# A decoder layer on one core: the pool mixer's map as a plain float32 product, and the kernel's plan with other factors by stage

## The chip, the cores and the metric

The kernel runs on one core of a Trainium2 chip, in one launch. The metric is the device time of an execution in microseconds. Three runs of the kernel before gave 1251.17, 1251.86 and 1253.36 us; their median is 1251.86. One more execution was profiled: its time is 1254.77 us, and its span, from the first to the last recorded instruction, 1252.9 us. All readings of the profile are from that one.

The engines are named PE (matrix products; PEld its weight loads), DVE (vector), ACT (scalar functions), POOL (a second vector engine, which also issues the accumulating transfers) and SP (issues the other transfers). Each has its own queue of instructions and runs it in order.

## The reference

One layer of a hybrid decoder for a prompt of 1024 tokens and 8 single tokens of other sequences (1032 columns in all), everything in float32, D = 1024:

```python
h = rmsnorm(x, g_mix)
u = h @ w_in                                    # a (512), val (512), gate (512)
ya = pool_mixer(a_ext, ...)                     # see below
yb = conv_mixer(val * sigmoid(gate), ...)       # depthwise width 31, LayerNorm, silu
x = x + concat([ya, yb]) @ w_out
x = x + cross_attn(rmsnorm(x, g_attn), mk, mv)  # 4 heads, 256 memory tokens; mk, mv = rmsnorm(mem) @ w_k, w_v
x = x + (silu(h @ w_gate) * (h @ w_up)) @ w_down   # h = rmsnorm(x, g_ffn)
```

The pool mixer, which the change touches, has four groups of 128 channels with trailing windows of 2, 4, 8 and 16 tokens:

```python
for g, w in enumerate((2, 4, 8, 16)):
    outs.append(win_sum[g] / minimum(w, pos + 1) - a[g])
y = einsum('blgc,gcd->blgd', d, w_map)          # a 128 x 128 map for each group
y = (y + b_map) * scale
```

The outputs are the final normalised states, the new pooling and convolution states, and the memory keys and values. The 8 single tokens attend to caches of their own, `cache_k` and `cache_v`.

## The kernel before

**Precision.** The kernel gives PE operands of the type float32r. To hold float32 accuracy it splits nearly every operand into a high and a low part, and every product is three products: high by high, high by low, low by high (`PASSES`, and `step3`, L449, with its matmuls at L457). Columns go in three pieces of 344, so one 128-channel block times one 128-row weight block is 9 matmuls of 344 columns. `split` (L338) makes the high part on ACT or POOL (L346 and L348) and the low part, operand minus high part, on DVE or POOL (L357). For weights there is another way, `split_by_dma` (L364): ACT makes the high part and its negated copy (L368; POOL can, L370), and then a transfer that POOL issues (L375) adds the weight from memory to the copy. POOL issues this transfer only when it reaches it in its queue.

**Weights.** They come as numbered blocks, `raw0`, `raw1`, ..., each loaded by SP into one of three buffers (tag "raw") and split into `w0`, `w1`, .... A raw buffer is free again once all parts of the split that read it are done, and only then can the block three further on be loaded. `NOT_BY_DMA` lists the blocks that are split by the engines, `LEAD` says how many blocks ahead the load and the split of a kind of weight are.

**Stages around the change.** The text `ORDER` names the pieces of the first half in the order in which their tasks are made. After the input projection PE runs the memory keys (`keys`, letters K) and values (`values`, V): K0 and K1 give `kT0`, V1 and V0 give `vv1` and `vv0`, K2 and K3 give `kT1`. Each takes two or four weight blocks: w12 to w15 for K0 and K1, w16 to w19 for V1, w20 to w23 for V0, w24 and w25 for K2. This text calls K2 the third key group. The pool mixer (`windows`, W, L777, and `mixer_out`, M, L841) is laid among them: the window sums `win` in doubling steps on DVE or POOL, the mean on DVE (L802 to L804), the split of the result `dop` (L807, L808), on PE the product `pmap` with the map, which is weight block 26 of the ring above, on ACT the evacuation `yf` (L848) with bias and scale, and its split `opa`. Then `oa` multiplies `opa` by the first rows of w_out, and `ob` the convolution's results `opb` by the others.

Later come the queries, and the attention: scores `sc`, softmax `probs`, their transposes `pt` and `pT`, the product with the values `pv`, whose results are evacuated as `oo` (high part on ACT, L1062, low part on DVE, L1063, in two pieces of 512 columns). Between them DVE does the attention of the 8 single tokens, as dot products with the cache (L1097), named `spcache_k3_0_4` and so on for keys or values, head, half and first token, with the broadcast query or probability row `sbcache`, and a small softmax (`sst`, `prow`). `po` (w_o times `oo`) follows, then the feed-forward in gated stages, its down projections, and the last stage.

**What sets the order.** No order of instructions is written out. Every piece of work is a task, `add(engines, emit, r, w)`: the engines that may do it, each with a cost in microseconds, and what it reads and writes. `Program.order()` then plays the tasks through: again and again it takes the engine that can start earliest, and on it the ready task of the highest priority (the one made first, by and large), and notes when the task ends, by its cost. Buffers are part of it: 2 PSUM buffers for the large products (tag "mm"), 3 raw, 2 w, 3 scratch, 19 operands. A group that needs a buffer gets the one that comes free first. So the costs decide which engine does a task and in which place of its queue it stands; on the chip the queues then run in the order that came out, whatever the real times are.

The costs of the kernel before are formulas in columns (`act`, `dve`, `pool_tt`, `pool_ts`) and single numbers for PE; from the down projections on, DVE's base is raised:

```python
fixed["DVE"] = 0.148
```

## Time and profile before

| what | us |
|---|---|
| median of three runs | 1251.86 |
| profiled execution | 1254.77 |
| its span | 1252.9 |
| PE busy | 1215.9 (97%) |
| DVE busy | 926.7 (74%) |
| ACT busy | 529.7 (42%) |
| POOL busy | 458.8 (37%) |

A row of a timeline gives the start in us from the span's start, the duration, the engine, the line, the operation, and what it writes and reads, with buffer numbers left out; "x9" means nine instructions in a row. A bracket tells how long the engine had been idle before, and which instruction or transfer ended that. In the rows of stretches stand the stretch, PE's busy time with its count, the granted TensorE clock (1.00 is full), the share of the transfer engines, and GB/s. "DMA to landing" is the time from a transfer's issue to its last byte.

### The profile page before, as it was taken

Reading aid. Unit: us, or ns where it says so; the run is one execution under the profiler, and the core shown is the slowest. Engines: PE = TensorE matmul, PEld = TensorE weight load, DVE = VectorE, ACT = ScalarE, POOL = GpSimd, SP = SyncE. Lnnn points to the kernel's source line nnn. Section 1 sums busy time; section 2 is a strip of 40 time slices with the busy share of each in tenths; the row PEclk is TensorE's granted clock in tenths of the full one; section 3 lists DMA queues with packets and bytes.
Section 4 is the critical chain, followed back from the end, with each engine's and each line's share of the span. In section 5 each row is a group of like instructions: output and inputs, shape, how many; then the busy total and the mean of one; then the engine's idle time right before and its main releaser. Section 6 shows DMA issues by size and latency. Waiting matters only on the chain.

```text
span 1252.9 us, 22090 instructions
## 1 busy us (share of the span) xinstructions
PE 1215.9 (97%) x8958; PEld 1194.3 (95%) x8958; DVE 926.7 (74%) x1564; ACT 529.7 (42%) x731; POOL 458.8 (37%) x407
## 2 busy tenths in 40 slices
PE   8999996999999999999999999999999999999996
PEld 8999976999999879999999999999999999999996
DVE  7899988657367777679778677866867887778644
ACT  7766648454223453344322222222222364433644
POOL 3577841021101002113422233133324477778401
PEclk9999997999999999999999999999999999999998
DMA  7447686734255664231331332223322597778703
GB/s 281 104 84 169 142 241 177 213 88 163 104 194 207 238 225 169 102 132 38 112 126 60 111 110 102 104 67 111 106 85 89 205 312 198 206 181 206 175 26 111
DMA packets 59157, 183.86 MB, mean 147 GB/s; under 512 B 7920, under 2 KB 11696, under 8 KB 57776
## 3 DMA queue, kind: packets, MB, share of 16 engines
q1 hardware_dynamic: 52288, 157.74, 36.4%
q0 software_dynamic: 6768, 24.72, 11.2%
q8 instruction: 70, 1.15, 0.4%
q14 instruction: 31, 0.25, 0.1%
HBM read 148.80 MB, written 33.64 MB: 146 GB/s over the span
## 4 chain that ended last, share of the span: by engine, by line
PE 73%; DVE 10%; issue 7%; DMA 5%; ACT 2%; POOL 2%; SPq 0%; DVEq 0%; POOLq 0%; ACTq 0%
PE pr L1290 45%; PE ps L457 11%; PE fd L1587 6%; PE oa L457 4%; PE ob L457 4%; DVE cacc L663 2%; DMA raw<-in_w_v 2%; PE sc L1000 1%; DVE spcache_v L1097 1%; DMA spcache_k<-in_cache_k 1%; POOL w L357 1%; PE pv L1058 1%; DVE spcache_k L1097 1%; DMA w<-in_w_in 1%; DVE xss L384 1%
## 5 line engine op out<-in xcount | busy, mean ns | idle before, releaser
L1305 DVE TENSOR_TENSOR su<-pr,su 128x258 f32<-128x258 f32 (+1 forms) x204 | 109.3, 558 | 71.0 <-PE pr L1290 69.9
L1290 PE MATMUL pr<-ab,wTa 128*128 128x258 f32 x1056 | 134.2, 283 | 0.8 <-DVE su L1305 0.8
L1290 PE MATMUL pr<-ab,wG 128*128 128x258 f32 x1056 | 133.9, 283 | 0.8 <-ACT wU L346 0.8
L1290 PEld LDWEIGHTS pr<-ab,wTa 128*128 128x128 f32 x1056 | 130.1, 189 | 1.0 <-issue 1.0
L1290 PEld LDWEIGHTS pr<-ab,wG 128*128 128x128 f32 x1056 | 129.8, 189 | 1.2 <-ACT wU L346 1.1
L1290 PE MATMUL pr<-ab,wTb 128*128 128x258 f32 x1056 | 130.6, 283 | 0.0
L1290 PEld LDWEIGHTS pr<-ab,wTb 128*128 128x128 f32 x1056 | 128.6, 190 | 0.0
L457 PE MATMUL ps<-xop,w 128*128 128x344 f32 x720 | 114.1, 320 | 0.3 <-DMA w<-in_w_in 0.3
L457 PEld LDWEIGHTS ps<-xop,w 128*128 128x128 f32 x720 | 113.3, 188 | 0.6 <-DMA w<-in_w_in 0.6
L1290 PE MATMUL pr<-hb,dV 128*128 128x258 f32 x768 | 98.5, 284 | 1.1 <-ACT pp L1309 0.7
L1290 PEld LDWEIGHTS pr<-hb,dV 128*128 128x128 f32 x768 | 95.0, 189 | 1.8 <-ACT pp L1309 0.9
L457 PE MATMUL ps<-xq,w 128*128 128x344 f32 x576 | 94.8, 321 | 0.0
L457 PE MATMUL po<-oo,w 128*128 128x344 f32 x576 | 91.0, 320 | 0.4 <-DVE oo L1063 0.4
L457 PEld LDWEIGHTS po<-oo,w 128*128 128x128 f32 x576 | 90.7, 188 | 0.7 <-DVE oo L1063 0.7
L457 PEld LDWEIGHTS ps<-xq,w 128*128 128x128 f32 x576 | 90.6, 188 | 0.1
L1305 DVE TENSOR_TENSOR x<-pr,x 128x516 f32<-128x516 f32 (+1 forms) x122 | 63.3, 556 | 23.2 <-PE pr L1290 22.0
L663 DVE SCALAR_TENSOR_TENSOR cacc<-glu,vec,cacc 128x511 f32<-128x511 f32 (+14 forms) x116 | 77.0, 742 | 0.0
L1290 PE MATMUL pr<-hb,dW 128*128 128x258 f32 x576 | 75.0, 283 | 0.2 <-DVE x L1305 0.2
L1290 PEld LDWEIGHTS pr<-hb,dW 128*128 128x128 f32 x576 | 71.7, 189 | 0.4 <-DVE x L1305 0.4
L1587 PE MATMUL fd<-ho,w 128*128 128x258 f32 x576 | 70.0, 283 | 0.0
L346 ACT ACTIVATE w<-raw 128x1024 fp32r<-128x1024 f32 (+2 forms) x34 | 31.6, 932 | 90.2 <-issue 38.2
L1587 PEld LDWEIGHTS fd<-ho,w 128*128 128x128 f32 x576 | 69.5, 189 | 0.1
(323 smaller groups left out, 2338.5 us busy)
## 6 DMA issues: line engine op xcount, KB each, us to landing
gr<-in_w_gu SPq DMA_DIRECT2D x44, 512.0 KB, 3.4
hs<-hb SPq DMA_DIRECT2D x28, 516.0 KB, 4.2
hb<-su SPq DMA_DIRECT2D x8, 1032.0 KB, 4.9
dr<-in_w_dn SPq DMA_DIRECT2D x16, 512.0 KB, 6.2
hb<-hb POOLq DMA_DIRECT2D x12, 516.0 KB, 7.8
spcache_k<-in_cache_k SPq DMA_DIRECT2D x12, 512.0 KB, 5.0
raw<-in_w_in SPq DMA_DIRECT2D x10, 512.0 KB, 5.3
w<-in_w_in POOLq DMA_DIRECT2D x9, 512.0 KB, 6.6
```

What stands on the lines that cost most here:

```text
L346: e.activation(dst(0), src(), AF.Copy, scale=1.0 if gain is None else gain)
L357: e.tensor_tensor(dst(1), src(), f32(dst(0)), ALU.subtract)
L384: add({"Pool": pool_tt(n), "DVE": dve(n)}, lambda e: e.tensor_tensor(total(), total(), sq[:, i, :n], ALU.add), [(sq, i), tkey], [tkey], lo ...
L457: e.matmul(ps[:, c, :CW], w[:, wi, cols], x[:, xi, c * CW : (c + 1) * CW], start=first and p == 0, stop=last and p == 2)
L663: e.scalar_tensor_tensor(acc[h][:, n:], src[:, : HALF - n], w, acc[h][:, n:], ALU.mult, ALU.add)
L1000: e.matmul(bank()[:, i * NMEM : (i + 1) * NMEM], qop[2 * h + dt][:, qi, tt * P : (tt + 1) * P], kk[:, ki, 2 * (h % 2) + dt], start=(dt == ...
L1058: e.matmul(ps[:, c], v[:, vi, m, col : col + P], pT[h][m][:, pi, sl], start=(m == 0 and p == 0), stop=(m == 1 and p == 2))
L1097: e.scalar_tensor_tensor(piece[:, b], piece[:, b], 1.0, bc[:, b], ALU.mult, ALU.mult, accum_out=out(m)[:, first + b : first + b + 1])
L1290: e.matmul(bank(c), w[:, wi, cols(j)], xs[0](j, xi)[:, c * TQ : (c + 1) * TQ], start=j == 0 and p == 0, stop=j == nj - 1 and p == 2)
L1305: from_sums(sums, "DVE", dve, lambda e, src, sl: e.tensor_tensor(as_banks(o(sl), src), src, as_banks(a(sl), src), ALU.add), [akey], [okey])
L1587: e.matmul(view(i), w[:, wi, col : col + P], hops[k][:, xi, lo + i * width // count : lo + (i + 1) * width // count], start=(k == 0 and p ...
```

## The change

The pool map is loaded once, by SP, into a buffer `wmap` of its own, and not split; it is no longer a block of the weights' ring, so every later block's number is one lower. The window results are not split either: `mixer_out` multiplies `win` by `wmap` as float32, with 3 matmuls of 344 columns for a group where it had 9. The evacuation `yf` and its split `opa` stay.

The plan's costs are written in another way: `pe` and `pe32` give PE's costs by columns, `MARGINS` scales or raises costs by the stage in which a task is made (early, gated, down, last), and POOL's base for two-operand work is 0.14 in place of 0.09. `ORDER` holds the same letters, in other lines. `BY_DMA` names, for each kind of weight, the blocks that are split with a transfer; apart from the map they are the ones that the old list left.

```diff
-NOT_BY_DMA = (0, 1, 2, 16, 18, 19, 22, 23, 26, 27, 35, 36, 53, 54)
-BY_DMA = ("w_in", "w_k", "w_v", "pool_map", "w_out_a", "w_out_b", "w_dn", "w_dn2")
+BY_DMA = {"w_in": (2, 3, 4, 5, 6, 7, 9, 10, 11), "w_k": (0, 1, 2, 3, 4, 5, 7), "w_v": (0, 1, 5), "w_out_a": (0, 1, 2, 3), "w_out_b": (0, 1), "w_dn": (17, 18, 19), "w_dn2": (1,)}
-LEAD = {"w_k": 4, "w_v": 3, "pool_map": 1, "w_out_a": 3, "w_q": 5, "w_in": 2, "w_out_b": 5, "w_o": 5}
+LEAD = {"w_k": 4, "w_v": 3, "w_out_a": 3, "w_q": 5, "w_in": 2, "w_out_b": 5, "w_o": 5}
...
+MARGINS = {
+    "early": {"PE": (0.93, 0.0)},
+    "gated": {},
+    "down": {"DVE": (1.0, 0.083)},
+    "last": {"PE": (0.93, 0.0), "DVE": (1.0, 0.083)},
+}
...
-        t.engines = engines
+        t.engines = {}
+        for e, cost in engines.items():
+            factor, more = self.margin.get(e, (1, 0)) if not nbytes else (1, 0)
+            t.engines[e] = cost * factor + more
...
+    def pe(n, count=1):
+        return (0.006 + 0.00044 * n) * count
+
+    def pe32(n):
+        return 0.01 + 0.0017 * n
...
     def pool_tt(n):
-        return 0.09 + 0.00216 * n
+        return 0.14 + 0.00216 * n
...
+    wmap = op_buf("wmap", (P, 512))
...
+        if not dops:
+            dma(lambda: wmap[:], lambda: io["pool_map"][0], 512 * 512, w=[(wmap,)])
...
-        dops[g] = op_r(f"dop{g}")
-        split(lambda p: dops[g][:, p], lambda p: (dops[g], p), cur, T, [ck])
+        dops[g] = cur, ck
...
-        if not opa:
-            state["wm"] = w_take("pool_map")
-        wmap, wmk = state["wm"]
         ps = mm_buf(f"pmap{g}")
-        step3(ps, wmap, wmk, block_cols(g), dops[g], 0, True, True)
+        cur, ck = dops[g]
+
+        def emit(e):
+            for c in range(NCH):
+                e.matmul(ps[:, c, :CW], wmap[:, block_cols(g)], cur()[:, c * CW : (c + 1) * CW], start=True, stop=True)
+
+        add({"PE": NCH * pe32(CW)}, emit, [(wmap,), ck], all3(ps))
...
-            fixed["DVE"] = 0.148
+            pg.margin = MARGINS["down"]
```

Other costs mean another order on every engine. PE's list is nearly the same (one map product stands one group later, a few small swaps); POOL's, ACT's and DVE's are changed in many places. Three of them follow.

**POOL, where the weights of K1, V1 and V0 are made ready.** A row is a line of the code, an operation, what it writes and what it reads; "DMA w17<-in_w_v" is the accumulating transfer of block 17, L357 (now L371) a low part. Before:

```order
L375 DMA w17_1544<-in_w_v 128x1024
L357 TENSOR_TENSOR w18_1565<-raw18_1486,w18_1565 128x1024
L357 TENSOR_TENSOR kT0_1640<-kf0_1628,kT0_1640 128x512
L357 TENSOR_TENSOR w19_1598<-raw19_1547,w19_1598 128x1024
L375 DMA w20_1622<-in_w_v 128x1024
L375 DMA w21_1699<-in_w_v 128x1024
L375 DMA w24_1760<-in_w_k 128x1024
```
Now:

```order
L371 TENSOR_TENSOR kT0_1651<-kf0_1627,kT0_1651 128x512
L389 DMA w17_1538<-in_w_v 128x1024
L371 TENSOR_TENSOR w18_1555<-raw18_1470,w18_1555 128x1024
L371 TENSOR_TENSOR w19_1596<-raw19_1542,w19_1596 128x1024
L389 DMA w20_1620<-in_w_v 128x1024
L371 TENSOR_TENSOR kT0_1651<-kf1_1697,kT0_1651 128x512
L389 DMA w21_1695<-in_w_v 128x1024
L371 TENSOR_TENSOR w22_1735<-raw22_1699,w22_1735 128x1024
L371 TENSOR_TENSOR w23_1746<-raw23_1712,w23_1746 128x1024
L371 TENSOR_TENSOR vv1_1802<-vf1_1787,vv1_1802 128x1024
L389 DMA w24_1764<-in_w_k 128x1024
```
The low part of `kT0` from `kf0` now stands ahead of block 17's transfer, where it stood behind it; that from `kf1` has come to POOL, ahead of block 21's; and the low parts of blocks 22 and 23 (DVE's before) are on POOL, and with `vv1`'s they stand ahead of block 24's transfer, which stood right behind block 21's.

**DVE, the mixer's last results, on the way to the first `oa`.** `win2` are the window sums of a group and then, by L804 (now L818), its mean; `opa` are the low parts of the mixer's results, `y2` and `ysum` the convolution's. Before, from the mean of `win2`:

```order
L804 SCALAR_TENSOR_TENSOR win2_1943<-win2_1943,a1_523 128x1032
L357 TENSOR_TENSOR w27_1947<-raw27_1774,w27_1947 128x1024
L357 TENSOR_TENSOR dop2_2018<-win2_1943,dop2_2018 128x1032
L357 TENSOR_TENSOR opa3_1995<-yf3_1976,opa3_1995 128x1032
L646 TENSOR_TENSOR y2_1082<-y2_1082,cp_593 128x507
L357 TENSOR_TENSOR opa1_2013<-yf1_2007,opa1_2013 128x1032
L646 TENSOR_TENSOR y2_1082<-y2_1082,cp_593 128x506
L682 TENSOR_TENSOR ysum_1203<-ysum_1203,y2_1082 128x1032
L646 TENSOR_TENSOR y2_1082<-y2_1082,cp_593 128x505
L357 TENSOR_TENSOR opa0_2030<-yf0_2015,opa0_2030 128x1032
L831 TENSOR_TENSOR kf3_2106<-kps3_2023,side_206 128x512
```
Now, from the low part of `opa3`:

```order
L371 TENSOR_TENSOR opa3_1975<-yf3_1969,opa3_1975 128x1032
L816 TENSOR_TENSOR win2_1971<-win2_1971,cnt_74 128x2x8
L817 TENSOR_REDUCE win2_1971<-side_206 128x8
L818 SCALAR_TENSOR_TENSOR win2_1971<-win2_1971,a1_523 128x1032
L657 TENSOR_TENSOR y2_1026<-y2_1026,cp_593 128x506
L371 TENSOR_TENSOR opa1_1983<-yf1_1980,opa1_1983 128x1032
L657 TENSOR_TENSOR y2_1026<-y2_1026,cp_593 128x505
L693 TENSOR_TENSOR ysum_1482<-ysum_1482,y2_1026 128x1032
L657 TENSOR_TENSOR y2_1026<-y2_1026,cp_593 128x504
L371 TENSOR_TENSOR opa0_2018<-yf0_2004,opa0_2018 128x1032
```
The low part of `dop2` is gone from between the mean and the results, as those of the three other groups are from further up, and `opa3` is ahead of the mean. Further up, the new list has from the third key group's end `kf2`, the sums of `win0`, the first of `win2`, the mean of `win0`, two more sums of `win2` (the second one was POOL's) around the low part of `kT1`, and then the rows above; in the old list the sums and the mean of `win0` came before `kf2`.

**DVE, the end of the attention.** `oo7` and `oo6` are the low parts of the last two products `pv`, the long names dot products with the cache. Before:

```order
L1097 SCALAR_TENSOR_TENSOR spcache_k3_0_4_4358,ssc_81<-spcache_k3_0_4_4358,sbcache_k3_4_4344 128x256 x4
L1097 SCALAR_TENSOR_TENSOR spcache_k3_1_4_4369,ssc_81<-spcache_k3_1_4_4369,sbcache_k3_4_4344 128x256 x4
L1063 TENSOR_TENSOR oo7_4403<-pv7_4385,oo7_4403 128x512 x2
L1118 TENSOR_REDUCE sst3_4443<-ss3_4431 8x1
L1119 SCALAR_TENSOR_TENSOR sst3_4443<-sst3_4443,r16_78 8x1
L1063 TENSOR_TENSOR oo6_4415<-pv6_4396,oo6_4415 128x512 x2
L1126 RECIPROCAL sst3_4443<-sst3_4443 8x1
L1127 TENSOR_SCALAR prow3_4447<-prow3_4447,sst3_4443 8x256
L1097 SCALAR_TENSOR_TENSOR spcache_v2_0_0_4252,os_80<-spcache_v2_0_0_4252,sbcache_v2_0_4417 128x256 x8
```
Now:

```order
L1079 TENSOR_TENSOR oo7_4359<-pv7_4349,oo7_4359 128x512
L1113 SCALAR_TENSOR_TENSOR spcache_v2_0_0_4208,os_80<-spcache_v2_0_0_4208,sbcache_v2_0_4329 128x256 x8
L1113 SCALAR_TENSOR_TENSOR spcache_k3_0_4_4333,ssc_81<-spcache_k3_0_4_4333,sbcache_k3_4_4320 128x256 x4
L1113 SCALAR_TENSOR_TENSOR spcache_k3_1_4_4336,ssc_81<-spcache_k3_1_4_4336,sbcache_k3_4_4320 128x256 x4
L1113 SCALAR_TENSOR_TENSOR spcache_v2_1_0_4211,os_80<-spcache_v2_1_0_4211,sbcache_v2_0_4329 128x256 x4
L1134 TENSOR_REDUCE sst3_4408<-ss3_4405 8x1
L1135 SCALAR_TENSOR_TENSOR sst3_4408<-sst3_4408,r16_78 8x1
L1113 SCALAR_TENSOR_TENSOR spcache_v2_1_0_4211,os_80<-spcache_v2_1_0_4211,sbcache_v2_0_4329 128x256 x4
L1142 RECIPROCAL sst3_4408<-sst3_4408 8x1
L1143 TENSOR_SCALAR prow3_4417<-prow3_4417,sst3_4408 8x256
L1079 TENSOR_TENSOR oo7_4359<-pv7_4349,oo7_4359 128x512
L1079 TENSOR_TENSOR oo6_4386<-pv6_4368,oo6_4386 128x512 x2
```
The second low part of `oo7` stood behind the dots of `k3`; it now stands behind those and the sixteen dots of `v2`, and the small softmax of head 3.

38 lines of the change are left out of this document (18 added, 20 removed), and 8 rows, old and new, of the table ORDER.

## The prediction

> **What bounds the kernel now.** I read the page first, then TensorE's own line of work, then what the engines that feed it did in its gaps.
>
> ```profile
> PE 1215.9 (97%) x8958; PEld 1194.3 (95%) x8958; DVE 926.7 (74%) x1564; ACT 529.7 (42%) x731; POOL 458.8 (37%) x407
> ```
>
> PE is busy for 97% of 1252.9 us, so 37 us at most can be won by filling its gaps, and everything else must come from less PE work. The question is only where PE stands still, and where it will stand still under the other order. The timeline of PE (start, duration, group, and in brackets the idle time ahead of it with what ended it) shows the gaps that the edit can reach:
>
> ```profile
> 115.83 33.31 PE L457 MATMUL ps<-xop,w 128*128 128x344 f32 x210 [0.30 <-DMA w<-in_w_in]
> 160.44 22.27 PE L901 MATMUL vps<-w,memg 128*128 128x512 f32 x96
> 187.98 2.86 PE L827 MATMUL kps<-memg,w 128*128 128x256 f32 x22 [1.86 <-DMA w<-in_w_k]
> 193.22 1.83 PE L457 MATMUL pmap<-dop,w 128*128 128x344 f32 x9 [2.37 <-ACT vf L906]
> 199.95 5.31 PE L457 MATMUL pmap<-dop,w 128*128 128x344 f32 x18 [4.91 <-ACT yf L848]
> 205.10 2.99 PE L827 MATMUL kps<-memg,w 128*128 128x256 f32 x24
> 215.84 15.80 PE L457 MATMUL oa<-opa,w 128*128 128x344 f32 x81 [3.02 <-ACT yf L848]
> 231.48 1.88 PE L868 MATMUL mean_ps<-ysum,ones_c 128*128 128x512 f32 x4
> 268.22 45.36 PE L457 MATMUL ob<-opb,w 128*128 128x344 f32 x288
> ...
> 430.76 3.03 PE L1058 MATMUL pv<-pT,vv 128*128 128x512 f32 x12 [0.83 <-DVE qs L978]
> 458.95 1.66 PE L1058 MATMUL pv<-pT,vv 128*128 128x512 f32 x6
> 461.21 4.40 PE L1058 MATMUL pv<-pT,vv 128*128 128x512 f32 x18 [0.60 <-DVE oo L1063]
> 465.45 0.38 PE L1110 MATMUL ss<-ident,ssc 128*8 128x128 f32 x2
> 466.25 90.97 PE L457 MATMUL po<-oo,w 128*128 128x344 f32 x576 [0.42 <-DVE oo L1063]
> ```
>
> The largest gaps, 10.3 us together (2.37, 4.91, 3.02), lie in the pool mixer, between the end of the third key group (190.84) and the first oa matmul (215.84). The chain there goes through ACT: the values' evacuation, the splits of the mixer's operands, the evacuation yf. Behind the attention PE hardly waits: 0.42 us before the 91 us of po. A gap has a second price, shown by the granted clock by stretch (PE busy us, count in brackets, then clock):
>
> ```profile
> 195.00:200.00 5.00, 0.09 (x2) 0.50 0.89 229
> 212.00:216.00 4.00, 0.98 (x8) 0.89 0.68 237
> 216.00:220.00 4.00, 4.00 (x15) 0.50 1.01 219
> 430.00:450.00 20.00, 16.27 (x109) 1.00 0.72 258
> ```
>
> After the gaps of 4.91 and 3.02 us the next work ran at half clock: 18 mixer matmuls took 5.31 us where 18 x 0.159 = 2.86 were due (an oa row at full clock: 288 ob matmuls in 45.36, 0.158 each), a loss of 2.5; and the 81 oa matmuls took 15.80 for 12.8, a loss of 3.0. The gaps up to 1.5 us between 430 and 450 left the clock at 1.00. [...]
>
> **The change, part by part.** I take nine terms, each against the profiled 1252.9 us.
>
> *The mixer's own arithmetic.* The split of the four operands goes:
>
> ```profile
> L346 ACT ACTIVATE dop<-win x4: 1047/1052/1069, 166.4 to 206.4; 128x1032 fp32r<-128x1032 f32 x4
> L357 DVE TENSOR_TENSOR dop<-win,dop x4: 1227/1229/1234, 167.6 to 207.5; 128x1032 fp32r<-128x1032 f32 x4
> ```
>
> That is 4.2 us of ACT and 4.9 us of DVE, besides the split of the map itself. On PE nine split matmuls (1.43 per group) become three plain float32 ones. The mean_ps row prices those: its four records are two matmuls of 512 columns, in 1.88 us with the tail of the last, thus some 0.88 each, 0.59 at 344 columns, 1.75 per group: 0.3 more, 1.2 over four groups. It is inside the mixer's term below.
>
> *1. The start of the input projection.* One row of POOL:
>
> ```profile
> 106.49 2.42 POOL L695 TENSOR_TENSOR t<-t,Rx 128x1032 f32<-128x1032 f32 x1 [0.74 <-ACT t L694]
> ```
>
> This product no longer stands ahead of a weight's accumulating DMA, so the 0.30 gap at 115.83 goes: **-0.3** (0 to -0.3).
>
> *2. The value and key weights.* Here the new order costs. These rows are of POOL, then of ACT, then of the accumulating DMAs as a whole:
>
> ```profile
> 153.21 0.87 POOL L375 DMA_DIRECT2D w<-in_w_v  x1
> 158.35 1.30 POOL L357 TENSOR_TENSOR kT<-kf,kT 128x512 fp32r<-128x512 f32 x1 [1.83 <-ACT kT L346]
> 182.13 1.23 POOL L375 DMA_DIRECT2D w<-in_w_k  x1
> ```
> ```profile
> 156.69 1.06 ACT L368 ACTIVATE w<-raw 128x1024 fp32r<-128x1024 f32 x1 [0.18 <-DMA raw<-in_w_v]
> 157.66 0.61 ACT L346 ACTIVATE kT<-kf 128x512 fp32r<-128x512 f32 x1
> 158.18 1.05 ACT L368 ACTIVATE w<-w 128x1024 fp32r<-128x1024 f32 x1
> ```
> ```profile
> DMA to landing us min/median/max: 5.5/7.2/10.5
> ```
>
> Weight w17's DMA is issued at 153.21 now. In the new order the low part of kT0 stands ahead of it on POOL; that waits for ACT's high part, which now stands behind both of w20's operations: ACT 156.69 + 1.0 + 1.0 + 0.6 = 159.3, POOL to 160.7, DMA at about 160.8. The DMA of 182.13 let PE go at 187.98, 5.85 later; so w17 lands at 166.6. PE wants it twelve value matmuls after 160.44, at 160.44 + 12 x 0.232 = 163.2: a wait of 3.4. Behind w17 wait w18's and w19's low parts, so the buffers of their raw blocks come free later, and w21 is some 1 us late; w24's DMA stands behind two more low parts and vv1's, which itself waits for the delayed values. I place the end of the third key group at 194.6, not 190.84: **+3.8** (0 if the DMAs land in time, to +6 if each takes the median 7.2). The wait of 3.4 is one that can halve the clock; part of that loss is swallowed by the waits for w21 and w24 behind it: **+1.0** (0 to +3).
>
> [...]
>
> *3. The mixer.* With the operands' splits gone, DVE sets the pace after the key group. Rows of DVE that price its list:
>
> ```profile
> 197.91 1.22 DVE L791 TENSOR_TENSOR win<-win 128x1022 f32<-128x1022 f32 x1
> 199.04 0.69 DVE L831 TENSOR_TENSOR kf<-kps,side 128x512 f32<-128x512 f32 x1
> 202.38 1.23 DVE L804 SCALAR_TENSOR_TENSOR win<-win,a 128x1032 f32<-128x1032 f32 x1
> 208.65 1.23 DVE L357 TENSOR_TENSOR opa<-yf,opa 128x1032 fp32r<-128x1032 f32 x1
> 209.79 0.68 DVE L646 TENSOR_TENSOR y<-y,cp 128x507 f32<-128x507 f32 x1
> ```
>
> From that key group to the low part of opa0 the new list has six 512-wide steps of sums and keys at 0.69, three full-width sums and adds at 1.22, two means at 1.5 with their small parts, three low parts of opa at 1.23 and three y steps at 0.68, with small copies: 17.0 us by durations, 15.6 from start to start (209.79 follows 208.65 after 1.14), and 1.2 before the first of them is under way. I find no wait in it (yf3, yf1, yf0 and their high parts on ACT fit beside it). So the first oa matmul comes about 16.8 after the key group, where it came 25.0 after it: **-8.2**, from 194.6 to 211.4. PE's work in between is 4 x 1.75 + 5.8 = 12.8, so 4.0 of idle stays, some 2.0 ahead of the third map product and 2.0 ahead of oa. Bounds: -10.3 if all three gaps close, -4 if the list on DVE loses 4 to waits for ACT.
>
> *4. The clock behind it.* A gap of 2.0 lies between 1.5 (no loss) and 3.02 (3.0 lost), nearer the first: **-2.0** (0 to -3.0).
>
> *5. ob.* The low part of opb1 now stands behind the last oa result on DVE, one operation of 1.23: **+1.2** (0 to +1.2).
>
> *6. Scores.* The query's low part comes ahead of a group of dots; the 0.83 gap at 430.76 goes: **-0.8**.
>
> *7. The end of the attention.* DVE again:
>
> ```profile
> 461.67 0.42 DVE L1097 SCALAR_TENSOR_TENSOR spcache_k<-spcache_k,sbcache_k 128x256 f32<-128x256 f32 x1
> ...
> 464.16 0.42 DVE L1097 SCALAR_TENSOR_TENSOR spcache_k<-spcache_k,sbcache_k 128x256 f32<-128x256 f32 x1
> ...
> 464.90 1.29 DVE L1063 TENSOR_TENSOR oo<-pv,oo 128x512 fp32r<-128x512 f32 x2 [0.31 <-ACT oo L1062]
> 466.11 0.40 DVE L1118 TENSOR_REDUCE sst<-ss 8x1 f32<-8x256 f32 x1
> ```
>
> Eight dots start 0.35 apart. po0 takes the PSUM buffer of pv7, which is free when both low parts of oo7 are done: 466.2, and PE starts at 466.25. In the new order the second oo7 stands behind 24 dots (16 of v2, eight of k3) and the short softmax steps sst3 and prow3. From the first oo7 at about 461.5: 0.65 + 24 x 0.35 + 1.0 for the softmax steps (the reduction above 0.40, three smaller) + 0.65 = 10.7, so po0 starts at about 472.4, with a little for the chain's hops: **+6.2**. Cover there is none: every po matmul needs that buffer. It could be 0 if po0's buffer came from elsewhere, and +8.5 if v2's broadcast lands late, since the dots then hold the whole queue.
>
> *8. The clock again.* PE idles for over 6 us, but for two short transposes, so the first po matmuls run at half clock: **+2.5** (0 to +3), the loss seen after 4.91.
>
> *9. The rest.* In the feed-forward's groups the last column is what PE waited over all their matmuls:
>
> ```profile
> L1290 PE MATMUL pr<-ab,wTb 128*128 128x258 f32 x1056 | 130.6, 283 | 0.0
> L1290 PE MATMUL pr<-hb,dV 128*128 128x258 f32 x768 | 98.5, 284 | 1.1 <-ACT pp L1309 0.7
> ```
>
> There is next to nothing to win, and PE's list there is nearly the same: **0** (-1 to +2).
>
> Sum: -0.3 + 3.8 + 1.0 - 8.2 - 2.0 + 1.2 - 0.8 + 6.2 + 2.5 = +3.4: a span of 1256.3. The profiled execution took 1254.77, the median of the runs is 1251.86; so on the median's scale 1251.86 + 3.4 = **1255.3**.
>
> **The rivals.** [...] (c) *Slower by far: the weight queue decides.* w17, w21 and w24 each take the median 7.2 us and PE runs half of the values at half clock: term 2 is +6 and +3, the broadcast of v2 is late (+8.5, +3), and the sum -0.3 + 9 - 8.2 - 2.0 + 1.2 - 0.8 + 11.5 = +10.4: 1262.3. It decides once w17's DMA is issued later than 157.4 (163.2 - 5.85). (d) *The change does nothing that can be seen*: PE's list is nearly the same rows, and if the waits balance, 1252.
>
> **How the numbers follow.** Forecast 0.43, (a) 0.24, (b) 0.14, (c) 0.12, (d) 0.07. The likeliest case by itself reaches from 1251 to 1260 by its bounds. Faster or slower is counted from 0.2%, or 2.5 us, about what a measurement here can tell. Slower: 0.37 of the forecast's 0.43, all of (c), 0.03 of (b) and (d) = 0.52. Faster: 0.23 of (a), 0.06 of (b) and (d) = 0.29. No change: the 0.19 that is left. The range of 1246.5 to 1262 takes in the forecast, (b), (d), most of (a), and (c) up to its middle.
>
> **What would show it.** Right: a gap of 3 us or so on PE inside the value products, ended by a DMA of w from in_w_v; the first oa matmul 16 to 18 us after the third key group; map products of 0.58 us per 344 columns; a gap of 6 us ahead of po, ended by DVE's oo, with dots of v2 ahead of it on DVE, and 0.50 granted behind it. Wrong in step 2: no gap in the values, and the key group's end at 191. Wrong in step 3: DVE waiting for ACT between win2 and opa0. Wrong in step 7: po beginning within 2 us of the last pv. If po's gap is absent and the rest holds, the kernel is about 5 us faster (3.4 - 8.7), and the forecast has the wrong sign.

## The result, and the profile after

The changed kernel took 1265.6 us (median of 6 runs, 1262.05 to 1269.7), the kernel before 1252.53 in its 6 runs beside it (1251.17 to 1253.69). The ratio is 1.0111, 95% interval 1.0099 to 1.0123: 13 us slower. The forecast was 1255.3 with a range up to 1262. The profiled execution took 1265.67, its span is 1263.9, 11.0 more than before; the other 2 us of the medians' difference come from the profiled execution of before, which lay 2.2 above the median of its 6 runs. What follows is made against the spans.

The page's first part, of the kernel after:

```profile
PE 1218.6 (96%) x8946; PEld 1193.0 (94%) x8946; DVE 920.7 (73%) x1576; ACT 520.7 (41%) x723; POOL 449.9 (36%) x393
```

PE is busy for 2.7 us more, and the rest of the 11.0 is idle time of PE. The timeline of PE after shows where, in the same stages as in the prediction:

```profile
160.07 3.89 PE L917 MATMUL vps<-w,memg 128*128 128x512 f32 x16
165.08 8.60 PE L917 MATMUL vps<-w,memg 128*128 128x512 f32 x36 [1.13 <-DMA w<-in_w_v]
174.07 10.38 PE L917 MATMUL vps<-w,memg 128*128 128x512 f32 x44 [0.39 <-DMA w<-in_w_v]
...
188.03 8.11 PE L840 MATMUL kps<-memg,w 128*128 128x256 f32 x46 [3.34 <-DMA w<-in_w_k]
195.98 3.63 PE L860 MATMUL pmap<-win,wmap 128*128 128x344 f32 x12
201.03 1.97 PE L860 MATMUL pmap<-win,wmap 128*128 128x344 f32 x6 [1.41 <-DVE win L818]
...
211.74 13.05 PE L468 MATMUL oa<-opa,w 128*128 128x344 f32 x81 [1.30 <-ACT yf L864]
...
307.50 12.78 PE L468 MATMUL ps<-xq,w 128*128 128x344 f32 x80
...
440.94 1.65 PE L1074 MATMUL pv<-pT,vv 128*128 128x512 f32 x6 [1.79 <-DVE pT L1060]
...
455.41 4.47 PE L1074 MATMUL pv<-pT,vv 128*128 128x512 f32 x18 [0.75 <-ACT oo L1078]
462.17 0.27 PE L1126 MATMUL ss<-ident,ssc 128*8 128x128 f32 x1 [2.29 <-DVE spcache_k L1113]
463.46 0.38 PE L1126 MATMUL ss<-ident,ssc 128*8 128x128 f32 x1 [1.02 <-DVE spcache_k L1113]
467.78 93.41 PE L468 MATMUL po<-oo,w 128*128 128x344 f32 x576 [3.94 <-DVE oo L1079]
...
562.01 5.30 PE L1306 MATMUL pr<-ab,wG 128*128 128x258 f32 x42 [0.82 <-ACT wU L360]
```

Two rows of before that the prediction did not show, for the comparison:

```profile
313.41 16.87 PE L457 MATMUL ps<-xq,w 128*128 128x344 f32 x106
...
558.04 5.28 PE L1290 MATMUL pr<-ab,wG 128*128 128x258 f32 x42 [0.83 <-ACT wU L346]
```

The reader is to see that the first half goes nearly as forecast. The values wait for w17 (1.13) and the keys for w24 (3.34). The first oa product starts at 211.74 (forecast 211.4, before 215.84), 15.6 us after the third key group's end at 196.14, and it runs at full clock. The queries' product starts 5.9 earlier than before. Behind the last pv stands the gap ahead of po (2.29, 1.02 and 3.94 around two short transposes). At the first gated product the kernel is 562.01 - 558.04 = 4.0 behind, where the sum said 3.4. The granted clock by stretch (columns as in the prediction) has the two half-speed pieces, behind w24's wait and behind the gap ahead of po, and none behind the mixer's gaps of 1.41 and 1.30 (1.00 in every stretch from 196 to 224):

```profile
188.00:192.00 4.00, 3.97 (x18) 0.50 1.04 308
...
216.00:220.00 4.00, 4.00 (x27) 1.00 0.99 318
...
468.00:472.00 4.00, 4.00 (x15) 0.50 0.64 242
```

The other 7.0 us of the 11.0 come behind that point, where the forecast had nothing. From the first gated product to the first product of the down projections (hb) both kernels take 448 us, and from the first product of the last stage (fd) to the end 82. The 6.7 lie between these, in the down stage: 1006.27 to 1170.89 before, 164.6, and 1010.41 to 1181.69 after, 171.3. These are the groups of products there, PE's waits ahead of them in the last column, of after and then of before:

```profile
L1306 PE MATMUL pr<-hb,dV 128*128 128x258 f32 x768 | 98.9, 284 | 3.8 <-DVE x L1321 1.6 <-ACT pp L1325 1.4 <-ACT x L1325 0.8
L1306 PE MATMUL pr<-hb,dW 128*128 128x258 f32 x576 | 75.4, 284 | 3.7 <-DVE x L1321 2.5 <-DVE su L1321 0.9 <-DVE pp L1321 0.3
```
```profile
L1290 PE MATMUL pr<-hb,dW 128*128 128x258 f32 x576 | 75.0, 283 | 0.2 <-DVE x L1305 0.2
```

With the 1.1 of dV that the prediction quoted, PE waited 1.3 us there before and waits 7.5 after. The gaps of after in the timeline of PE, one by one, are all short and ended by several engines:

```profile
1010.41 1.68 PE L1306 MATMUL pr<-hb,dW 128*128 128x258 f32 x12 [0.88 <-DVE su L1321]
...
1038.79 3.18 PE L1306 MATMUL pr<-hb,dV 128*128 128x258 f32 x24 [1.15 <-DVE x L1321]
1048.54 1.71 PE L1306 MATMUL pr<-hb,dV 128*128 128x258 f32 x12 [0.78 <-ACT x L1325]
...
1055.11 1.72 PE L1306 MATMUL pr<-hb,dW 128*128 128x258 f32 x12 [2.48 <-DVE x L1321]
```

On POOL, in the groups by line between 1000 and 1130 us, the accumulating transfers of hb now wait for ACT's negated copies, first after and then before:

```profile
L389 POOL DMA_DIRECT2D hb<-hb x12 | 10.9, 952 | 5.9 <-ACT hb L382 5.9
```
```profile
L375 POOL DMA_DIRECT2D hb<-hb x12 | 10.6, 951 | 0.0
```

POOL reaches these transfers before ACT has made their operands, and stands; dt and dV, the next weights of the down stage, queue behind.

### The profile page after: what moved, and what is told of

Read it like the earlier page. It is cut to its first block, busy times and chain, and to the rows that moved or that the text cites. A ratio compares the mean times of both kernels' runs of the same rounds, so it can differ in the third digit from the quotient of the medians.

```text
span 1263.9 us, 22051 instructions
## 1 busy us (share of the span) xinstructions
PE 1218.6 (96%) x8946; PEld 1193.0 (94%) x8946; DVE 920.7 (73%) x1576; ACT 520.7 (41%) x723; POOL 449.9 (36%) x393
## 3 DMA queue, kind: packets, MB, share of 16 engines
q8 instruction: 70, 1.15, 0.4%
## 4 chain that ended last, share of the span: by engine, by line
PE 86%; DVE 5%; DMA 5%; issue 2%; ACT 2%; POOL 1%; SPq 0%; DVEq 0%; ACTq 0%; POOLq 0%
PE pr L1306 43%; PE ps L468 15%; PE po L468 7%; PE fd L1605 6%; PE oa L468 4%; PE ob L468 3%; PE sc L1016 2%; PE pv L1074 1%; DMA hs<-hb 1%; DMA raw<-in_w_v 1%; PE kps L840 1%; DMA x<-x2d 1%; PE psg L468 1%; PE psv L468 1%; DVE hb L371 1%
## 5 line engine op out<-in xcount | busy, mean ns | idle before, releaser
L1306 PE MATMUL pr<-ab,wG 128*128 128x258 f32 x1056 | 134.2, 283 | 0.8 <-ACT wU L360 0.8
L1306 PE MATMUL pr<-ab,wTa 128*128 128x258 f32 x1056 | 134.1, 283 | 0.0
L1306 PEld LDWEIGHTS pr<-ab,wG 128*128 128x128 f32 x1056 | 130.1, 190 | 1.1 <-ACT wU L360 1.1
L1306 PE MATMUL pr<-ab,wTb 128*128 128x258 f32 x1056 | 130.3, 283 | 0.0
L1306 PEld LDWEIGHTS pr<-ab,wTa 128*128 128x128 f32 x1056 | 130.0, 190 | 0.0
L1306 PEld LDWEIGHTS pr<-ab,wTb 128*128 128x128 f32 x1056 | 128.3, 190 | 0.0
L1306 PE MATMUL pr<-hb,dV 128*128 128x258 f32 x768 | 98.9, 284 | 3.8 <-DVE x L1321 1.6
L1306 PEld LDWEIGHTS pr<-hb,dV 128*128 128x128 f32 x768 | 95.0, 189 | 4.9 <-DVE x L1321 2.0
L1306 PE MATMUL pr<-hb,dW 128*128 128x258 f32 x576 | 75.4, 284 | 3.7 <-DVE x L1321 2.5
L1306 PEld LDWEIGHTS pr<-hb,dW 128*128 128x128 f32 x576 | 71.9, 190 | 4.6 <-DVE x L1321 2.7
L1306 PE MATMUL pr<-ab,wU 128*128 128x258 f32 x528 | 67.2, 283 | 0.0
```

The costliest lines, as they stand in the source:

```text
L1306: e.matmul(bank(c), w[:, wi, cols(j)], xs[0](j, xi)[:, c * TQ : (c + 1) * TQ], start=j == 0 and p == 0, stop=j == nj - 1 and p == 2)
```

## The experiments

The theory after the result (**A**): the plan's new costs, not the plain map, make the kernel slower, at two places that are independent of each other: the low parts of oo at the end of the attention (predicted), and the order of the down stage, through the one number in it that costs POOL's two-operand work 0.05 us more. Rivals: (**B**) the down stage is longer because the plain map shifts what reaches it; (**C**) it is the rewritten PE and DVE costs of that stage. Line numbers move by a few from kernel to kernel; L1306, L1308 and L1292 are the same matmul. In the table the starts of po and of the first gated product, and the length of the down stage from the first hb to the first fd product, are from each one's timeline of PE.

| kernel | median us | ratio to before [95%] | po | gated | down stage |
|---|---|---|---|---|---|
| before | 1252.53 | | 466.25 | 558.04 | 164.6 |
| after | 1265.60 | 1.0111 [1.0099, 1.0123] | 467.78 | 562.01 | 171.3 |
| 1 after, late cost back | 1259.97 | 1.0054 [1.0041, 1.0066] | 471.16 | 564.33 | 165.0 |
| 2 before, late cost alone | 1261.74 | 1.0071 [1.0057, 1.0086] | 464.94 | 556.77 | 172.5 |
| 3 after, cost back from the down stage on | 1264.55 | 1.0093 [1.0080, 1.0106] | 467.00 | 561.21 | 170.7 |
| 4 after, oo first | 1258.42 | 1.0044 [1.0032, 1.0057] | 459.18 | 553.11 | 171.6 |
| 5 before, plain map alone | 1248.84 | 0.9975 [0.9960, 0.9990] | 460.78 | 552.71 | 164.8 |
| 6 after, map split again | 1275.18 | 1.0175 [1.0155, 1.0195] | 477.94 | 571.13 | 170.6 |
| 7 after, kT0 on DVE | 1267.84 | 1.0121 [1.0101, 1.0142] | 467.77 | 562.24 | 173.1 |
| 8 after, two low parts on POOL | 1265.44 | 1.0108 [1.0090, 1.0126] | 467.77 | 562.09 | 171.6 |
| 9 after, four transfers later | 1265.24 | 1.0091 [1.0077, 1.0105] | 467.97 | 562.35 | 169.9 |
| 10 plain map alone, kT0 on DVE | 1258.70 | 1.0046 [1.0033, 1.0058] | 470.16 | 561.90 | 164.7 |
| 11 after, both mends (1 and 4) | 1250.89 | 0.9982 [0.9973, 0.9992] | 459.48 | 553.62 | 164.8 |
| 12 number 9, and low parts behind sums | 1263.54 | 1.0086 [1.0071, 1.0101] | 466.99 | 561.26 | 168.9 |

**1 to 3: the late cost.** POOL's base of 0.14 is put back to 0.09 for all tasks made from the gated stage on; then 0.14 is put into the kernel before from the same point; then 0.09 in the changed kernel from the down stage on only.

```diff
-        return 0.14 + 0.00216 * n
+        return pool_base["tt"] + 0.00216 * n
...
     rsqrt_rows("Rf", Rf, RF, xss2, [(xss2,)], ones_d, 0, T)
+    pool_base["tt"] = 0.09
```

> The changed kernel with POOL's two-operand base set back to 0.09 from the gated stages on (0.14 stays in the early part). Up to there its lists are those of the changed kernel row for row; from there on they are nearly those of the kernel before. Theory A (the dearer POOL in the plan of the late stages is the loss behind the attention): from the start of the first gated product the span takes 695 us as before, in place of 702; time about 1258.5 (1257 to 1260), still some 6 above the kernel before. Rival B (the early part hands over something, late loads or buffers, that slows the late stages whatever their order): the late part stays near 702 and the time near 1265.

> The kernel before with POOL's two-operand base raised from 0.09 to 0.14 from the gated stages on, and nothing else. Its early lists are those of the kernel before row for row, its late lists nearly those of the changed kernel. Theory A: the early part takes 558 us as before and the late part 702 in place of 695: 1259.5 (1258 to 1262). Rival B: the late part stays at 695 and the time at 1252.5.

> The changed kernel with POOL's base set back to 0.09 only from the down projections on; early and gated lists stay those of the changed kernel. If the loss is made by the order of the down projections alone: about 1258.5, as with the base set back from the gated stages on. If the changed order in the gated stages, the way in which it enters the down projections, makes it: near 1265. The down projections' list here is neither that of the kernel before nor that of the changed one, so a value between is possible.

The down stage follows this number and nothing else: 165.0 with 0.09 in the changed kernel, 172.5 with 0.14 in the kernel before. The kernel before with that one number changed, and its old map, is 9.1 us slower, and POOL's wait appears with it (groups by line, 1000 to 1130 us):

```profile
L377 POOL DMA_DIRECT2D hb<-hb x12 | 10.9, 958 | 6.5 <-ACT hb L370 6.1 <-PE pr L1292 0.4
```

So A holds for the late part and B and C fall. In the third run, the cost back from the down stage's own tasks on leaves 170.7. Either most of the loss is in what the plan has already laid out with the gated stage's costs when these tasks are made, or its lists, which are neither those of before nor those of after, are as bad for a reason of their own; which of the two is not shown. Number 1's median falls by 5.6, its part from the first gated product to the end by 6.6 (695.3 for 701.9). The start of the gated stage is scatter of single executions: the kernels whose lists up to there are those of after (after, 1, 3, 8, 9, 12) reach it between 561.21 and 564.33. Which of the new costs moves the rows of the first half was not tried.

**4: oo first.** The second low part of oo7 and those of oo6 get priority over the dots on DVE.

```diff
+            if n in (6, 7):
+                pg.first.append(low)
...
+        for t in self.first:
+            t.prio -= 1000
```

> The changed kernel with the low parts of oo6 and oo7 given the first place on DVE at the end of the attention, ahead of the dots of v2 and k3; elsewhere only a few rows move. If the 24 dots ahead of the last oo7 are the cost: the gap before po (2.29, 1.02 and 3.94 us around the two ss transposes) shrinks to under 1.5, po begins some 6 us earlier, and takes 91.0 us in place of 93.4 since the clock stays full: 1265.6 - 8.4 = 1257 (1256 to 1259). Rival: the dots that now come later delay the sample part of oo7 and with it the last piece of the first po, and half of the gain or more goes: 1261 or above.

In the timeline of PE, po starts at 459.18 with no gap ahead of it, and has two inside:

```profile
482.82 1.18 PE L470 MATMUL po<-oo,w 128*128 128x344 f32 x6 [0.47 <-DVE xa L1198]
485.01 15.22 PE L470 MATMUL po<-oo,w 128*128 128x344 f32 x95 [1.01 <-POOL w L373]
```

The two gaps take 1.5 back; the second is ended by POOL's low part of a weight that po now wants earlier. The median falls by 7.2, within the expected range, and in the profiled execution the first gated product comes 8.9 earlier (553.11). The predicted steps 7 and 8 are thereby shown as cause: they cost 9.7 us between the last pv and the end of po.

**5 and 6: the two halves of the change apart.** Number 5 is the kernel before with the plain map alone, the old costs and the old list of blocks, renumbered; number 6 is the changed kernel with the map split as before. The core of the first:

```diff
-        dops[g] = op_r(f"dop{g}")
-        split(lambda p: dops[g][:, p], lambda p: (dops[g], p), cur, T, [ck])
+        dops[g] = cur, ck
...
-        step3(ps, wmap, wmk, block_cols(g), dops[g], 0, True, True)
+        add({"PE": NCH * (0.01 + 0.0017 * CW)}, emit, [(wmap,), ck], all3(ps))
```

and of the second, the other way:

```diff
-        dops[g] = cur, ck
+        dops[g] = op_r(f"dop{g}")
+        split(lambda p: dops[g][:, p], lambda p: (dops[g], p), cur, T, [ck])
```

> The kernel before with the pool map as a plain float32 product and nothing else of the change: the old costs and factors stay. Only the lists from the value weights to the mixer's end differ from the kernel before; from there on they are the same row for row. Theory A (the product is the gain, the other factors are the loss): the oa products begin 4 us earlier and run at full clock, so everything behind them comes 6 us earlier, as it did in the changed kernel up to the end of the attention: 1246.5 (1245 to 1249). Rival C (the plain product itself costs, or its gain is taken back at the next wait): 1251 or above.

> The changed kernel with the map and its operands split into high and low parts again, nine products a group: the other costs and factors alone. From the end of the mixer on its lists are those of the changed kernel row for row. Theory A: it loses what the plain product gave, 6 us, and keeps the losses behind it: 1271.5 (1269 to 1274). Rival C: about 1265 or below.

By the medians the plain map is worth -4.2 with the old costs (1248.84 to 1253.02) and -9.6 with the new ones (1265.6 to 1275.18), while the new costs are worth +16.8 and +22.2. Number 5 is the fastest kernel of the study. It is inside its range, 2.3 above the time expected, and its timeline of PE shows why:

```profile
175.88 3.04 PE L904 MATMUL vps<-w,memg 128*128 128x512 f32 x12 [1.76 <-DMA w<-in_w_v]
...
191.10 7.22 PE L827 MATMUL kps<-memg,w 128*128 128x256 f32 x46 [3.42 <-DMA w<-in_w_k]
...
213.50 13.04 PE L455 MATMUL oa<-opa,w 128*128 128x344 f32 x81 [1.30 <-ACT yf L851]
```

The late value and key weights come with the map's removal too, not with the costs alone. Number 6 missed its range of 1269 to 1274 by 1.2: the plain map gave more there than the 6 us expected. The mixer's gaps of the kernel before are back, such as this one, beside those of the new order:

```profile
222.16 8.68 PE L471 MATMUL oa<-opa,w 128*128 128x344 f32 x36 [3.50 <-ACT yf L862]
```

**7 and 10: the weight queue.** The low parts of kT0 go to DVE, so that the transfer of w17 no longer waits behind them on POOL; once in the changed kernel, once in number 5.

```diff
-        if gain is None and not ps:
+        if gain is None and not ps and not dve_low:
             lo["Pool"] = pool_tt(n)
```

> The changed kernel with the low parts of kT0 kept to DVE, so that on POOL the accumulating DMA of w17 has nothing of the keys ahead of it, and that of w24 comes ahead of the low part of vv1. From the gated stages on its lists are those of the changed kernel. Theory (POOL's queue makes these weights late): no gap among the value products (1.13 and 0.39 now), the third key group ends near 191 in place of 196.1 and runs at full clock, and since DVE's list behind it moves with it, all that follows is 5 us earlier: 1260.6 (1259 to 1262.5). Rival (the weights are late because their raw blocks are): the gap of 3.34 stays and the time is 1264 or above.

> The kernel before with the plain map alone and the low parts of kT0 on DVE. In the run with the map alone PE waited 6.8 us for weights in the values and the third key group (0.77, 1.76, 0.83, 3.42). Theory (POOL's queue makes half of these): the waits in the values go, the one in the key group shrinks to 2 or so as it did by 2 us in the changed kernel, and DVE's list behind it moves along: 1248.8 - 3 = 1246 (1244 to 1248). Rival (what the key group gains is given back at the next DVE low part, as it was in the changed kernel): 1248.5.

Both missed. In number 7 the values run without a gap, and PE then waits longer for w24; from the timelines of PE and POOL:

```profile
160.07 22.32 PE L917 MATMUL vps<-w,memg 128*128 128x512 f32 x96
...
186.72 7.11 PE L840 MATMUL kps<-memg,w 128*128 128x256 f32 x46 [4.09 <-DMA w<-in_w_k]
```
```profile
176.82 0.89 POOL L389 DMA_DIRECT2D w<-in_w_k  x1 [0.30 <-POOL w L384]
```

The transfer was issued at 176.82 and released PE at 186.72, 9.9 later. The gap and the time are those of the rival, but not for its reason: ACT began on w24's raw block at 174.31, in after at 173.97, so the block was there; it was the transfer that took longer (in after PE began 7.2 behind the issue at 180.86), and why is open. The key group's end comes 2.3 earlier than in after (193.83 for 196.14), but the wait ahead of it has grown (4.09 for 3.34); number 10's expectation speaks of a shrunken wait. The first oa product starts 1.8 earlier (209.95), and behind three of them PE stops for DVE's opa (0.93). The first gated product comes at 562.24, as in after: the gain is given back. Number 10 is 9.9 slower than number 5, with larger waits in the values and the mixer; in its timeline of PE:

```profile
177.15 13.21 PE L904 MATMUL vps<-w,memg 128*128 128x512 f32 x44 [2.86 <-DMA w<-in_w_v]
...
206.24 7.88 PE L827 MATMUL kps<-memg,w 128*128 128x256 f32 x48 [4.99 <-ACT yf L851]
```

What one operation's engine does to the whole plan is larger than the operation. That w17's wait comes from kT0 on POOL is shown by number 7's 96 values without a gap; that mending it in this way would pay is refuted.

**8, 9 and 12: single rows of the down stage.** In number 8 the low parts hb1_1 and hb1_3, in a row on DVE ahead of the sums that release the 2.48 gap, are done by POOL. In number 9 only POOL's list is edited, behind the plan: the four transfers that waited for ACT go 2 to 6 places back, behind steps of dt. Number 12 adds to number 9 a move of the two low parts behind four sums on DVE.

```diff
+        if pool_low:
+            lo.pop("DVE")
```
```diff
+    for name, places in [((1, 6), 5), ((1, 0), 6), ((1, 5), 2), ((1, 4), 4)]:
+        k = next(i for i, (t, _) in enumerate(listed) if t is marked[name])
+        on_pool = [i for i in range(k + 1, len(listed)) if listed[i][1] == "Pool"][places - 1]
...
+        listed.insert(on_pool, listed.pop(k))
```
```diff
+    dve_moves = [((1, 1), 5), ((1, 3), 4)]
```

> The changed kernel with the low parts of two hidden blocks of the second chunk (hb1_3 and hb1_1) kept to POOL; only some rows around them move. Theory (two of them in a row on DVE, 4.6 us beside one on POOL, hold back the evacuations of PE's down products): the gap of 2.48 ended by DVE's x shrinks to under 0.5, with the half clock behind it; the gaps of 0.6 to 1.2 ahead of it stay: 1262.5 (1261 to 1264). Rival (the blocks themselves are late, and PE would wait for them next): the gap moves on, 1265 or above.

> The changed kernel with one edit in POOL's list and no other row moved: the four accumulating transfers of the second chunk's hidden blocks (hb1_4, hb1_5, hb1_0, hb1_6) stand behind the steps of dt1, dt2, dV2 and dV3, as they do in the kernel before, where POOL never waited ahead of them; in the changed kernel it waited 5.9 us there for ACT's copies, with the down weights dt queued behind. Theory (this wait makes the down weights late, and so PE's products and evacuations): POOL's wait ahead of them goes below 1.5, PE's gaps from 1010 to 1056 shrink from 6.7 to under 3 us, the part from the first gated product on takes 697 to 698 in place of 702: 1261 (1259 to 1263). Rival (the hidden blocks or the loads are late in themselves): the part stays at 701 or above, 1265.

> The changed kernel with the four transfers of hb1 moved on POOL as in the experiment before, and on DVE the two low parts hb1_3 and hb1_1 (4.6 us with POOL's work beside them) moved behind four sums of x2_3 that stood behind them. Both orders are else the changed kernel's. The first says that the 2.46 us gap on PE near 1052 us is those two low parts standing ahead of the sums: it goes, the part from the first gated product on falls from 700.35 to about 698, the median from 1265.2 to about 1263, and moves of a few rows then make up 4 of the 7 us. The second says, as when the low parts went to POOL, that the delay only moves on, because DVE has as much to do as before in that stretch: another gap of 1.5 us or more stands within 10 us behind, and the part stays at 700 or above.

Number 8 is a miss: with the two low parts off DVE, the delay reappears in the timeline of PE as two other gaps:

```profile
1048.53 1.71 PE L1308 MATMUL pr<-hb,dV 128*128 128x258 f32 x12 [2.01 <-ACT x L1327]
1051.88 0.58 PE L1308 MATMUL pr<-hb,dV 128*128 128x258 f32 x1 [1.64 <-DVE x L1323]
```

Number 9 takes POOL's wait away (the same twelve transfers: 10.9 us busy, idle 0.0) and with it the gaps of 1.15 and 0.78, and number 12 takes the gap of 2.46 behind them away, for which one of 1.76 comes at another place. The down stage falls by only 1.4 and then 1.0 of the 6.7, and number 9's time is that of its rival. These falls are near the scatter: the kernels with the lists of after in this stage (after, 4, 6 and 7) take 170.6 to 173.1 there. PE's idle time inside the stage tells more: 5.3 to 6.6 us in those four, 4.6 in number 9, 3.6 in number 12, 1.4 in the kernel before. The timelines of PE, of number 9 and then of number 12, show what ate the rest:

```profile
1052.86 2.10 PE L1308 MATMUL pr<-hb,dW 128*128 128x258 f32 x12 [2.46 <-DVE x L1323]
1054.76 4.20 PE L1308 MATMUL pr<-hb,dV 128*128 128x258 f32 x24
```
```profile
1050.37 3.05 PE L1308 MATMUL pr<-hb,dV 128*128 128x258 f32 x24
1055.17 4.87 PE L1308 MATMUL pr<-hb,dW 128*128 128x258 f32 x24 [1.76 <-DVE pp L1323]
```

24 products take 3.05 us at full clock. Behind the gap they took 4.20 in number 9 (and the 12 ahead of them 2.10, where after's took 1.72) and 4.87 in number 12, with the clock granted at 0.50 in both (1054 to 1056 in number 9, 1057 to 1059 in number 12): 1.5 and 1.8 lost, where after, behind its 2.48, lost nothing (1.00 from 1050 to 1062). Number 7, with the lists of after, lost some there: twelve dV products took 2.95 at 1051.43 and twelve dW 2.95 at 1055.51, where after's took 1.70 (at 1050.93) and 1.72, and PE was busy for 3.1 us more in its stage than in that of after. So in number 12 the gaps inside the stage are 3.6 us together, 2.2 more than the 1.4 before; with the 1.8 of the clock that is 4.0 of the 4.2 by which its stage is still longer. From the first gated product to the end it took 699.2, between the 698 of the one theory and the 700 of the other: part of the delay went, and part moved on. Which rows make the remaining gaps was not found; what is shown is the number that makes them.

**11: both mends.** Numbers 1 and 4 together.

> The changed kernel with two mends together: POOL's old base from the gated stages on, and the low parts of oo first at the end of the attention. If the two losses add up: 1265.6 - 5.6 - 7.2 = 1252.8 (1251 to 1255), within 0.2% of the kernel before, and above the 1248.8 of the map alone. If they overlap: 1256 or above.

The median of 1250.89, 14.7 below after and 0.18% below before, is about the sum: 5.6 and 7.2 of the medians, with a first half that is not disturbed (gated at 553.62). The two losses add up, as theory A says.

## Why the prediction was wrong

Its direction held, and so did the sum of its first eight terms (4.0 for 3.4). Single terms were off by up to 1.2, some up and some down, so that the sum came so near is in part luck. Its last term failed, and that by itself put the time outside the range. Each term as forecast, and as it reads from the rows above:

| step | forecast | measured | from |
|---|---|---|---|
| 1 start of the input projection | -0.3 | -0.4 | first value product, 160.07 for 160.44 |
| 2 weights late, and their clock | +4.8 | +5.7 | third key group's end, 196.14 for 190.84, less step 1 |
| 3 mixer | -8.2 | -9.4 | 15.6 for 25.0 from there to oa |
| 4 clock behind it | -2.0 | -2.8 | 81 oa products, 13.05 for 15.80 |
| 5 ob | +1.2 | +0.9 | queries, 307.50 for 313.41, less the above |
| 6 scores | -0.8 | +0.2 | last pv's end, 459.88 for 465.61 |
| 7 wait ahead of po | +6.2 | +7.3 | 7.9 for 0.6 from there to po |
| 8 clock in po | +2.5 | +2.4 | 93.41 for 90.97 |
| sum to the gated stage | +3.4 | +4.0 | 562.01 for 558.04 |
| 9 the rest | 0 (-1 to +2) | +7.0 | 701.9 for 694.9 to the end |

**Step 9, "The rest", is the step that failed.** It argued that PE's list is nearly the same and that PE waited next to nothing there before, and so set 0. Both premises are true and the conclusion does not follow. Idle time of 0.0 in the kernel before says that the other engines' lists fitted it, and it bounds what can be won, not what can be lost. The lists of POOL and DVE had changed, and the prediction walked through them only up to po. The runs show in its place that 0.05 us on POOL's base, from the gated stage on, lays out a down stage that is 6.7 us longer (numbers 1 and 2). One part of it could have been read: a transfer of hb ahead of the dt steps on POOL, with ACT's copy of hb late, is the same figure as w17 behind kT0 in step 2.

**Step 2** was right in its sum and wrong in the place of the large wait. w17's transfer was forecast to be issued at 160.8 and land 5.85 later; it was issued at 159.35 (POOL's timeline, below) and let PE go at 165.08, 5.7 later. PE did 16 products before it stopped and not the 12 of the forecast, so it waited 1.13 and not 3.4. The large wait and the half clock came at w24 instead (3.34). As the prediction says, its transfer, the first of the two at 180.86, stood behind vv1's low part; ACT's copies for it were ready at 176.1. The values were not late for that, as the prediction has it: ACT evacuates them at 176.03, and at 176.22 in the kernel before. The place in POOL's list alone made the transfer 4.2 later than before (last row):

```profile
159.35 0.88 POOL L389 DMA_DIRECT2D w<-in_w_v  x1
...
178.50 2.41 POOL L371 TENSOR_TENSOR vv<-vf,vv 128x1024 fp32r<-128x1024 f32 x1 [5.20 <-ACT vv L360]
180.86 1.79 POOL L389 DMA_DIRECT2D w<-in_w_k  x2
```
```profile
176.61 0.86 POOL L375 DMA_DIRECT2D w<-in_w_k  x1 [10.58 <-ACT w L368]
```

**Step 3**: the list on DVE ran as worked out, 15.5 from its first step (196.24) to the end of opa0's low part (211.74), without a wait for ACT; the 1.2 that the prediction put ahead of the first step was 0.1. The plain map takes 1.8 us per group (the 12 records of two groups in 3.63), as forecast. But what ended the wait ahead of oa was ACT's yf, as in the kernel before, which followed the last map product (210.47 to 211.69); DVE's opa0 was done at the same time. DVE set PE's pace as far as the third map product, and from there PE's own work and yf did as much; the prediction had DVE alone. **Step 6** failed by 1.0: other waits stand where the old one was, such as the 1.79 ahead of a pv. **Step 7** was right in its mechanism: these are DVE's rows around the 24 dots, in its timeline of after, and po starts when the first of the last three low parts is done:

```profile
457.18 0.69 DVE L1079 TENSOR_TENSOR oo<-pv,oo 128x512 fp32r<-128x512 f32 x1 [1.60 <-PE pv L1074]
457.79 0.41 DVE L1113 SCALAR_TENSOR_TENSOR spcache_v<-spcache_v,sbcache_v 128x256 f32<-128x256 f32 x1
...
467.05 1.87 DVE L1079 TENSOR_TENSOR oo<-pv,oo 128x512 fp32r<-128x512 f32 x3
```

Of the rivals, (a) and (b), at 0.24 and 0.14, count on weights that come sooner. Neither before nor after shows that: their accumulating transfers took at least 5.5 and 5.2 us from issue to landing, and both rivals fell with w24's wait (3.34). (d) fell with everything. (c) came near in its number, and its sign came too (w17's transfer issued later than 157.4), but the loss came by other means: half of the values did not run at half clock (1.00 from 160.07 to 184.4), and v2's broadcast was not late.

What stays open: which rows of the down stage make the gaps that numbers 9 and 12 left, and why the same lists of the first half end up to 3 us apart in single executions. Part of that is how fast PE ran: behind the same gap of 1.79 ahead of a pv, six products and the eight transposes after them took 2.18 and 1.91 in number 1, and 1.65 and 1.04 in after, where the granted clock was 1.00 from 440.94 to 450.

## What to carry to other kernels

Where an order comes out of a plan of costs, a change of one cost has to be read to the end of every engine's list, and most of all in the stages where nothing waits now: no idle time there means that the old order fits, and that another has nothing to win. Separate a mixed edit into its arithmetic and its plan before judging it: here the arithmetic alone is 4 us faster, and the costs that came with it took 17. Mending one row of such a list often moves the wait to the next one; a mend pays where the delayed result is the only thing that its reader waits for, as with oo.

## What was unexpected in the hardware

**The clock's gap.** The prediction had a full clock behind gaps up to 1.5 us and half of it behind 3.02 and 4.91. In these runs gaps between those were enough, but not always: behind 2.86 in number 10, 44 value products took 13.21, where they took 10.38 in after, and the clock was 0.50 from 177 to 180; behind number 9's 2.46 (0.50 from 1054 to 1056) and number 12's 1.76 the clock was halved, behind after's 2.48 it was not. The length of the gap alone does not decide it. These are stretches of number 12, whose gap ended at 1055.17, and then of after, whose gap ended at 1055.11:

```profile
1054.00:1055.20 1.20, 0.03 (x1) 1.00 0.99 344
1055.20:1056.00 0.80, 0.80 (x5) 1.00 0.93 325
1056.00:1057.00 1.00, 1.00 (x8) 0.57 0.95 334
1057.00:1058.00 1.00, 1.00 (x7) 0.50 0.44 178
1058.00:1059.00 1.00, 1.00 (x6) 0.50 0.93 197
1059.00:1060.00 1.00, 1.00 (x9) 0.72 0.87 316
1060.00:1062.00 2.00, 2.00 (x19) 1.00 0.98 357
```
```profile
1050.00:1054.00 4.00, 1.94 (x15) 1.00 0.80 259
1054.00:1056.00 2.00, 0.89 (x7) 1.00 0.39 62
1056.00:1058.00 2.00, 2.00 (x19) 1.00 1.00 411
1058.00:1062.00 4.00, 3.99 (x32) 1.00 0.53 170
```

In number 12 PE had begun again when the clock fell: it was still 1.00 up to 1056. What decides is not shown.

**Two low parts beside POOL.** In the timelines of DVE, two low parts of 128x1032 took 4.61 us in after, while POOL did a two-operand operation of the same size (1050.47, 2.56 long). The first of them took 1.23; the second began at 1050.65, took 3.47, and ended 1.1 after POOL's. In number 12, with POOL's done at 1049.70, they took 1.22 and 1.23:

```profile
1049.51 4.61 DVE L371 TENSOR_TENSOR hb<-hs,hb 128x1032 fp32r<-128x1032 f32 x2
```
```profile
1049.73 1.22 DVE L373 TENSOR_TENSOR hb<-hs,hb 128x1032 fp32r<-128x1032 f32 x1
...
1051.21 1.23 DVE L373 TENSOR_TENSOR hb<-hs,hb 128x1032 fp32r<-128x1032 f32 x1
```

POOL's 128x256 operation that began at 1051.43 in number 12, while DVE's second one ran, took 1.61; one of the same kind in after, at 1056.46, took 0.74. That the two engines' work side by side was the cause was not tried by itself.
